# TensorE's order in the first mixer written by hand: the recurrent heads and the attention become stages that advance between the contraction steps of the projections

## The chip, the core and the metric

The kernel runs on one core of one Trainium2 chip. The metric is device time in microseconds (us) of one execution, from three runs. Five engines matter: TensorE (PE) multiplies, VectorE (DVE), ScalarE (ACT) and GpSimd (POOL) work on vectors, and SyncE (SP) issues most of the DMAs (ACT issues the rest). Each takes its instructions strictly in order. An instruction whose data are not there holds up everything behind it on its engine.

## The reference, cut to what matters

A diffusion backbone of two layers over 256 latent tokens and 256 context tokens, 2048 features, in f32. The first layer's mixer has eight heads of a recurrent memory (gated delta rule, in chunks of 64, both directions of time) and beside them eight heads of attention to a neighbourhood on a grid; one input projection feeds both, one output projection takes both. The second layer's mixer is a short convolution. A gated feed-forward block follows each. The change lies in the first mixer.

```python
# gated delta rule, per chunk: M from k and decay, T = inverse of (I + M)
m = where(i > j, einsum(kb, k) * decay, 0)
t_inv = triangular_solve(eye + m, eye)
u = t_inv @ (v * beta);  w = t_inv @ (kb * exp(gc))
def step(s, xc):                       # from chunk to chunk, state s
    v_new = u_c - w_c @ s
    s_next = s * exp(gl_c) + kd_c.T @ v_new
    o_c = qd_c @ s + a_c @ v_new       # latent tokens only
```

k, q and v of these heads go through a convolution over five tokens and SiLU first. k and q are then scaled to length one and rotated. The context tokens are scanned first; their final state starts the scan of the latent tokens. The attention heads add a relative bias, and the recurrent heads' outputs are normalised and gated with a projection z.

## The kernel before, in words

**Projections as streams.** f32 products are made of three products of reduced-precision parts: a weight is split into whi (ACT, L170) and wlo (DVE L238 for the first 576 columns of 1024, POOL L240 for the rest), an activation into a high and a low part. A *stream* is one projection: it loads weights by SP (L227, tile raw), splits them, and for each of 16 contraction steps of 128 features issues its matmuls. `fm_stream` (L308) puts features on the partitions, with matmuls 256 wide: 24 in a step where latent and context tokens are both projected, 12 where only latent tokens are. `tm_stream` (L279, L280, L282) puts tokens on the partitions, with matmuls 512 wide: 12 in a step. The streams of the first mixer come in this order: KA0, KA1 (k of the recurrent heads, four heads each), QA0, QA1 (q), VA0, VA1 (v), QB0, QB1, KB0, VB0, KB1, VB1 (q, k, v of the attention), ZA (the gate z), WO0, WO1 (the output projection). In the profile shown they start at about 110, 147, 204, 244, 281, 341, 390, 428, 466, 534, 605, 688, 748, 853 and 930 us; WO1 ends at 978.5.

**Deferred work.** After a projection of recurrent heads, `head_evac` (L568) puts ten items into the list `later`; `drive` (L411) takes one from it after each contraction step of the next stream. `front` runs the convolution (ACT, then four steps on DVE at L560, SiLU on ACT at L562; tile cv). `back` turns its result with matmuls against an identity (L189, tile sm, four of 128x128), copies it (L170, tile hq), squares it on POOL (L590) and sums on DVE (L591). `done` makes the reciprocal roots (L213 to L218) and runs `normalise` on POOL (L606 scaling, L612 to L615 rotation) and DVE (L616, L617). For k it then writes the tile to memory (L630, kd). For q it turns it to features with L189 matmuls (`sm<-cs,hq`) and writes these.

**Recurrent heads.** `gates` makes decay factors. `chunk_matrices` loads k back from kd (L779, tile ktok), turns it (`gd<-cs,ktok`, L189), forms the products and decay masks (POOL L768 tile gm, PE L772, ACT L774 tile em, DVE L808 tile nt) and solves small triangular systems on DVE. `inverses` joins these into larger blocks on PE (L883, L896). `scan` carries the state (PE L921, L930, L941, L949, L963; DVE L924 tile R; ACT L945 tile vd, L959 tile vn). `latent_scores` makes the matrix AT (L996, L997). In the code all of this stands as straight calls: `chunk_matrices` and `inverses` ahead of QA0, the scans and `latent_quad` ahead of QB0.

**Attention.** `na_scores` loads a bias strip (issued by ACT, L1084, tile br with one buffer), adds a band mask on POOL (L1087, tile bq) and makes scores (L1091 and L1092). `na_values` turns the probabilities (L189, tile PT) and multiplies with v (L1115). Its tiles take the room of the context activations, which VB1 is the last to read. Eight heads, ahead of ZA in the code.

**Who orders the work.** A scheduler with a model of each instruction's time takes the whole program and orders every engine's instructions; the order in the code is only the order of the dependences. One thing is held: the first turning matmul of each convolved head keeps its place (`keep_in_program_order`, L586). Beside the streams a `Pump` advances jobs for modulation weights (`ada_job`; ACT L332, POOL L333, DVE L335) at rates R_QB, R_KB, R_ZA, R_WO per step.

## Time and profile before

| what | value |
|---|---|
| median of three runs | 2942.07 us (2934.33, 2942.07, 2943.47) |
| profiled execution, its own time | 2944.36 us |
| its span, first to last instruction | 2942.5 us |
| mean granted TensorE clock | 0.981 of full speed |
| first mixer from the start of KA1 to the end of WO1 | 146.7 to 978.5 us |

The rows that the prediction shows are read like this. In a window's row stand its length, then busy time and number of instructions of PE, PEld (weight loads), DVE, ACT and POOL, then the granted clock, the share of time in which the DMA engines were busy, and GB/s. In a row of waits stand engine, tile and line of what waited, what it waited for, the sum in us, how often, and the longest. In a timeline row stand start, duration, engine, line, operation, written and read tiles, shapes, count, and in brackets the idle time ahead of it and what ended it. In a group's row stand count, then busy time and mean ns of one, then idle time ahead. The matmuls of PE overlap: one's duration is longer than the distance to the next. An engine name with a q (ACTq, SPq) is a DMA's issue.

### The profile page before, as it was taken

Reading aid. Unit: us, or ns where it says so; the run is one execution under the profiler, and the core shown is the slowest. Engines: PE = TensorE matmul, PEld = TensorE weight load, DVE = VectorE, ACT = ScalarE, POOL = GpSimd, SP = SyncE. Lnnn points to the kernel's source line nnn. Section 1 sums busy time; section 2 is a strip of 40 time slices with the busy share of each in tenths; the row PEclk is TensorE's granted clock in tenths of the full one; section 3 lists DMA queues with packets and bytes.
Section 4 is the critical chain, followed back from the end, with each engine's and each line's share of the span. In section 5 each row is a group of like instructions: output and inputs, shape, how many; then the busy total and the mean of one; then the engine's idle time right before and its main releaser. Section 6 shows DMA issues by size and latency. Waiting matters only on the chain. (4 is left out here: it accounts for less than half of the span.)

```text
span 2942.5 us, 40694 instructions
## 1 busy us (share of the span) xinstructions
PE 2757.0 (94%) x15113; PEld 2292.6 (78%) x15113; DVE 1896.3 (64%) x2409; ACT 1335.1 (45%) x1822; POOL 587.1 (20%) x431
## 2 busy tenths in 40 slices
PE   5898998989899999999999999999999999999997
PEld 3688988878777778878877777777777888888886
DVE  3378766845566777666667867777767446445675
ACT  3245544333354444444445555453544444444554
POOL 1147535336322111110111101111101001000010
PEclk9999999999999999999999999999999999999999
DMA  9954567777767688877878766878568667656653
GB/s 344 297 156 115 159 196 242 240 225 222 218 191 245 236 290 287 301 265 260 274 252 274 261 198 239 296 259 301 196 193 294 194 186 257 187 186 217 191 193 122
DMA packets 284929, 680.80 MB, mean 231 GB/s; under 512 B 57273, under 2 KB 97313, under 8 KB 283323
## 3 DMA queue, kind: packets, MB, share of 16 engines
q1 hardware_dynamic: 262148, 652.48, 67.5%
q10 hardware_dynamic: 22583, 25.73, 2.9%
q8 instruction: 118, 1.93, 0.3%
q14 instruction: 80, 0.66, 0.1%
HBM read 657.63 MB, written 20.48 MB: 230 GB/s over the span
## 5 line engine op out<-in xcount | busy, mean ns | idle before, releaser
L238 DVE TENSOR_TENSOR wlo<-raw,whi 128x1024 fp32r<-128x1024 f32 (+1 forms) x800 | 1009.2, 1274 | 490.1 <-ACT whi L170 476.8
L170 ACT ACTIVATE whi<-raw 128x1024 fp32r<-128x1024 f32 x800 | 835.7, 1055 | 634.3 <-PE mm L282 449.5
L335 DVE SCALAR_TENSOR_TENSOR acc<-araw,cT,acc 128x1024 f32<-128x1024 f32 (+1 forms) x312 | 357.5, 1146 | 292.7 <-DMA araw<-in_ada_w_dram 252.4
L280 PE MATMUL mm<-wlo,fhi 128*128 128x512 f32 x1232 | 478.8, 394 | 3.6 <-DVE wlo L238 3.3
L279 PE MATMUL mm<-whi,fhi 128*128 128x512 f32 x1232 | 476.4, 397 | 0.0
L282 PE MATMUL mm<-whi,flo 128*128 128x512 f32 x1232 | 394.1, 393 | 0.0
L333 POOL TENSOR_TENSOR acc<-araw,acc 128x1024 f32<-128x1024 f32 (+1 forms) x78 | 155.7, 1996 | 1118.0 <-ACT araw L332 632.3
L280 PEld LDWEIGHTS mm<-wlo,fhi 128*128 128x128 f32 x1232 | 232.9, 189 | 57.8 <-DVE wlo L238 8.4
L282 PEld LDWEIGHTS mm<-whi,flo 128*128 128x128 f32 x1232 | 232.2, 189 | 50.2
L279 PEld LDWEIGHTS mm<-whi,fhi 128*128 128x128 f32 x1232 | 233.1, 189 | 48.6 <-ACT sg L1262 0.4
L279 PE MATMUL mm<-whi,ahi 128*128 128x512 f32 x672 | 262.1, 395 | 3.8 <-ACT ahi L173 2.0
L280 PE MATMUL mm<-wlo,ahi 128*128 128x512 f32 x672 | 261.8, 393 | 0.3 <-DVE wlo L238 0.3
L240 POOL TENSOR_TENSOR wlo<-raw,whi 128x448 fp32r<-128x448 f32 x112 | 160.2, 1432 | 279.8 <-ACT whi L170 259.8
L282 PE MATMUL mm<-whi,alo 128*128 128x512 f32 x672 | 211.5, 395 | 2.1 <-DVE alo L174 1.7
L332 ACT ACTIVATE araw<-araw,cT 128x1024 f32<-128x1024 f32 (+1 forms) x78 | 74.4, 954 | 301.0 <-DMA araw<-in_ada_w_dram 256.8
L308 PE MATMUL mm<-hllo,whi 128*128 128x256 f32 x640 | 184.6, 291 | 0.0
L308 PE MATMUL mm<-hlhi,wlo 128*128 128x256 f32 x600 | 172.1, 291 | 4.5 <-DVE wlo L238 4.5
L308 PE MATMUL mm<-hlhi,whi 128*128 128x256 f32 x600 | 170.2, 293 | 1.2 <-DVE hlhi L506 1.2
L1159 POOL TENSOR_TENSOR xs<-rtmp,xs 128x512 f32<-128x512 f32 x24 | 35.4, 1496 | 631.4 <-DVE rtmp L1157 631.4
L279 PEld LDWEIGHTS mm<-whi,ahi 128*128 128x128 f32 x672 | 126.8, 189 | 32.2 <-ACT ahi L173 2.8
L282 PEld LDWEIGHTS mm<-whi,alo 128*128 128x128 f32 x672 | 126.2, 189 | 32.2 <-DVE alo L174 5.1
L280 PEld LDWEIGHTS mm<-wlo,ahi 128*128 128x128 f32 x672 | 126.7, 189 | 29.4 <-DVE wlo L238 1.9
(398 smaller groups left out, 4677.6 us busy)
## 6 DMA issues: line engine op xcount, KB each, us to landing
araw<-in_ada_w_dram SPq DMA_DIRECT2D x288, 512.0 KB
raw<-in_ffn_w_down_dram SPq DMA_DIRECT2D x176, 512.0 KB
raw<-in_ffn_w_gate_dram SPq DMA_DIRECT2D x160, 512.0 KB
raw<-in_ffn_w_up_dram SPq DMA_DIRECT2D x160, 512.0 KB
raw<-in_ev_w_in_dram SPq DMA_DIRECT2D x112, 512.0 KB
araw<-in_ada_w_dram SPq DMA_DIRECT2D x192, 256.0 KB
raw<-in_od_w_in_dram SPq DMA_DIRECT2D x96, 512.0 KB
raw<-in_ev_w_out_dram SPq DMA_DIRECT2D x32, 512.0 KB
```

Source lines behind the costliest of these rows:

```text
L170: ACT.activation(dst, src, AF.Copy)
L238: DVE.tensor_tensor(lo[:, 0:cut], raw[:, 0:cut], hi[:, 0:cut], op=OP.subtract)
L240: POOL.tensor_tensor(lo[:, cut:], raw[:, cut:], hi[:, cut:], op=OP.subtract)
L279: PE.matmul(ps[ti][n], a, hi[:, n * 512:(n + 1) * 512], start=first, stop=False)
L280: PE.matmul(ps[ti][n], a, lo[:, n * 512:(n + 1) * 512], start=False, stop=False)
L282: PE.matmul(ps[ti][n], b, hi[:, n * 512:(n + 1) * 512], start=False, stop=last)
L308: PE.matmul(ps[f][:, n * 256:(n + 1) * 256], wt, mv(w, k), start=False, stop=i == len(ks) - 1 and g == len(group) - 1 and j == 2 and w == ...
L332: ACT.activation(raw, raw, AF.Copy, scale=col)
L333: POOL.tensor_tensor(acc2, raw, acc2, op=OP.add)
L335: DVE.scalar_tensor_tensor(acc, raw, col, acc, op0=OP.mult, op1=OP.add)
L1159: eng.tensor_tensor(v, tmp, v, op=OP.add)
```

## The change

From the end of KA0 to the end of WO1, PE's instructions keep the order in which the code issues them (`tc.manual_schedule` for PE alone); the scheduler still orders the other engines. To set that order, the code is rewritten:

- `gates`, `chunk_matrices`, `inverses`, `scan`, `latent_scores` and `latent_quad` become generators that yield between stages, joined in `recurrent`. `drive` advances this chain by `pace` stages after each contraction step: 0.5 during KA1, 0.55 during QA, 0.8 during VA, 0.5 during QB, 1.1 during KB and VB. What is left when VB1 ends is issued there (`chain.finish`).
- In `scan` the two directions of time are issued together in each stage. In `chunk_matrices` and `latent_scores` the mask gm is made a stage ahead of its matmuls.
- The attention becomes a generator, advanced by 1.7 stages in each step of ZA. The loads of a head are issued two heads ahead of its scores, except for head 0 and head 1. Scores, turning and values are stages of their own; the score tiles alternate between the two PSUM pools for every head (GH is gone).
- The recurrent heads' outputs (`latent_out`) become stages in WO (one per step). YO, the order of contraction in WO, is (2, 3, 0, 1) instead of (2, 0, 1, 3).
- The turning of q to features comes three deferred steps later, as two items (`features`).
- The pump's rates: R_KB 1.8 to 1.9, R_ZA 1.8 to 3.0. An `ada_job` of the mixer yields twice more ahead of its own PE work (lag).

The set of instructions is the same; their order differs. The lines of the changed code stand up to 75 further down.

```diff
+S_KA, S_QA, S_VA, S_QB, S_KB, S_ZA, S_WO = 0.5, 0.55, 0.8, 0.5, 1.1, 1.7, 1.0
...
-    def drive(stream, pump=None, n=1):
+    def drive(stream, pump=None, n=1, chain=None, pace=0):
         for _ in stream:
             if later:
                 f, args = later.pop(0)
                 f(*args)
+            if chain:
+                chain(pace)
...
+            for _ in range(3):
+                defer(lambda: None)
             for g in range(2):
+                defer(features, qt, g)
...
+    order = Stack()
+    order.enter_context(tc.manual_schedule(engines={mybir.EngineType.PE}))
...
             ktok = load_tok("ktok", kd, t0, q)
             kT = g4("kT", "kT").rearrange("p (h t) -> p h t", h=4)
+            yield
             to_features(kT, ktok, gdt)
...
+                gm = [masked(d, t0 + ti, q) for d in range(2)]
+                yield
...
+    def recurrent():
+        yield from gates()
+        parts = yield from chunk_matrices(1)
+        xdTs = []
+        for q in range(2):
+            xdTs.append((yield from inverses(parts, q)))
+        parts = yield from chunk_matrices(0)
+        for q in range(2):
+            yield from scan(q, 1, xdTs[q])
...
+    chain = Pump([recurrent()], 1, 1)
+    drive(fm_stream([(wv, C_KA + 512, 512)], ks, [0, 1], ka_evac(1)), None, 0, chain, S_KA)
...
+    def attention():
+        loads = {0: na_loads(0)}
+        yield
+        loads[1] = na_loads(1)
+        held = na_scores(0, *loads.pop(0))
+        vb = na_values(0)
+        for h in range(8):
+            yield
+            if h < 6:
+                loads[h + 2] = na_loads(h + 2)
+            ahead = na_scores(h + 1, *loads.pop(h + 1)) if h < 7 else None
+            yield
+            PT = na_turned(h, held)
+            vnext = na_values(h + 1) if h < 7 else None
+            yield
+            na_out(h, vb, PT)
+            held, vb = ahead, vnext
```

Three places in the order follow.

**PE, where the second half of the keys comes back** (heads 4 to 7, loaded as ktok). Before, this stands in the stream VA0:

```order
L308 MATMUL mm<-hlhi,whi 128x256
L308 MATMUL mm<-hchi,whi 128x256
L308 MATMUL mm<-hllo,whi 128x256
L189 MATMUL gd<-cs,ktok 128x128 x8
L189 MATMUL sm<-cs,hq 128x128 x6
L308 MATMUL mm<-hclo,whi 128x256
```

Now it stands in QA0. The row of four `sm<-cs,cv` is the last turned head of KA1; 24 stream rows stand between the two rows with gm, and 12 behind the second, of which the last three are shown.

```order
L190 MATMUL sm<-cs,cv 128x128 x4
L824 MATMUL gd<-kT 128x128 x4
L789 MATMUL gd<-cs,gm 128x128 x4
...
L789 MATMUL gd<-cs,gm 128x128 x4
...
L309 MATMUL mm<-hlhi,whi 128x256
L309 MATMUL mm<-hllo,whi 128x256
L309 MATMUL mm<-hlhi,wlo 128x256
L190 MATMUL gd<-cs,ktok 128x128 x8
L309 MATMUL mm<-hlhi,whi 128x256
```

The turning of ktok has moved from VA0, two streams after KA1, to 36 stream matmuls after KA1's last convolved head.

**POOL, at the same keys** (sq are squares, hq the keys, rope the rotation, gm masks, n_... copies for the inverses, wlo the weights' low parts). Before:

```order
L590 TENSOR_TENSOR sq<-hq 128x256
L606 TENSOR_TENSOR hq<-hq,rkr 128x512 x4
L240 TENSOR_TENSOR wlo<-raw,whi 128x448
L612 TENSOR_TENSOR rope<-hq,cs 128x256
L613 TENSOR_TENSOR rope<-hq,cs 128x256
L590 TENSOR_TENSOR sq<-hq 128x256
```

Now:

```order
L595 TENSOR_TENSOR sq<-hq 128x512
L840 COPY n_1845<-nt 32x128 x2
L781 TENSOR_TENSOR gm<-cs,g_t 128x512 x2
L241 TENSOR_TENSOR wlo<-raw,whi 128x448
L840 COPY n_1845<-nt 32x128 x2
L611 TENSOR_TENSOR hq<-hq,rkr 128x512 x4
L617 TENSOR_TENSOR rope<-hq,cs 128x256
L618 TENSOR_TENSOR rope<-hq,cs 128x256
```

The scaling of these keys now comes directly behind their own last squares with two masks, a weight's low part and four copies between; before, it stood among the squares of the queries (128x256), a stream later.

**PE, at the start of ZA** (kb, qb and bq are an attention head's keys, queries and bias). Before:

```order
L1091 MATMUL sm<-kb,qb 128x512 x2
L279 MATMUL mm<-whi,hlhi 128x512 x4
L949 MATMUL gd<-vd,ktok 128x128 x2
L280 MATMUL mm<-wlo,hlhi 128x512
L949 MATMUL gd<-vd,ktok 128x128
...
L963 MATMUL gd<-vn,AT 128x128 x4
L1092 MATMUL sm<-bq,cs 128x256 x2
```

Now, after the first 24 matmuls of ZA:

```order
L1163 MATMUL gd<-kb,qb 128x512
L1164 MATMUL gd<-bq,cs 128x256
L1163 MATMUL sm<-kb,qb 128x512
L1164 MATMUL sm<-bq,cs 128x256
L1163 MATMUL gd<-kb,qb 128x512
L1164 MATMUL gd<-bq,cs 128x256
L1163 MATMUL sm<-kb,qb 128x512
L1164 MATMUL sm<-bq,cs 128x256
L345 MATMUL sm<-cs,acc 128x1 x4
L280 MATMUL mm<-whi,hlhi 128x512
```

The scores of head 0 and of head 1 now stand in one group with no stream matmul between, and the last steps of the scan have moved ahead of ZA.

## The prediction

> **What bounds the kernel now.** I read the page first:

> ```profile
> PE 2757.0 (94%) x15113; PEld 2292.6 (78%) x15113; DVE 1896.3 (64%) x2409; ACT 1335.1 (45%) x1822; POOL 587.1 (20%) x431
> ```

> TensorE is busy for 94% of the span, and the change alters none of its work. So only three things can move the end: PE's idle time, its clock, and work of others that comes too late for it. The windows of the first mixer say how much there is. They are cut at KA1 to VA, QB to VB, and ZA to WO:

> ```profile
> 146.70:389.50 242.80, 224.92 (x1803) 221.32 (x1802) 192.91 (x340) 119.69 (x180) 134.28 (x130) 0.96 0.48 144
> 389.50:748.40 358.90, 321.37 (x3067) 293.58 (x3066) 225.35 (x365) 131.94 (x231) 165.36 (x138) 0.97 0.74 227
> 748.40:978.50 230.10, 213.91 (x1041) 171.75 (x1039) 148.17 (x253) 107.14 (x188) 63.41 (x49) 0.98 0.72 226
> ```

> Length less PE's busy time gives 17.9, 37.5 and 16.2 us of idle time, 71.6 us together. The clock column adds 242.8 × 0.04 + 358.9 × 0.03 + 230.1 × 0.02 = 25 us at most. So nothing can be worth more than 97 us, 3.3% of the span. PE's waits in the same windows name what it waits for. First part:

> ```profile
> PE sm L189 <- ACT cv L562: 12.6, 8, 2.8
> PE mm L308 <- DVE wlo L238: 1.7, 1, 1.7
> PE sm L698 <- ACT abs L170: 1.5, 1, 1.5
> PE gd L189 <- DMA ktok<-kd: 1.5, 1, 1.5
> ```

> Middle:

> ```profile
> PE gd L941 <- ACT state L170: 3.9, 1, 3.9
> PE gd L772 <- DVE AT L997: 3.3, 1, 3.3
> PE gd L941 <- DVE R L924: 3.0, 1, 3.0
> ...
> PE gd L772 <- POOL gm L768: 2.3, 3, 0.8
> ```

> End:

> ```profile
> PE sm L1092 <- POOL bq L1087: 2.7, 1, 2.7
> PE sm L1115 <- ACT PT L165: 2.6, 2, 1.8
> ...
> PE gd L930 <- DMA qT<-qTd: 1.2, 1, 1.2
> ```

> No wait is longer than 4 us. The scheduler puts a step of the heads where its data are there, and the idle time is many small misses. The change swaps this for a fixed order, so the sum asks two things at each place: how long is the chain of other engines, and how much PE work stands between its start and its end.

> **The prices of a matmul.** At the start of QB the timeline of PE shows both clocks:

> ```profile
> 402.50 1.22 PE L308 MATMUL mm<-hlhi,wlo 128*128 128x256 f32 x4 [2.83 <-DVE wlo L238]
> ...
> 403.74 0.41 PE L308 MATMUL mm<-hllo,whi 128*128 128x256 f32 x1
> 403.95 0.41 PE L308 MATMUL mm<-hlhi,wlo 128*128 128x256 f32 x1
> ...
> 405.80 0.28 PE L308 MATMUL mm<-hlhi,wlo 128*128 128x256 f32 x1
> 405.92 0.28 PE L308 MATMUL mm<-hlhi,whi 128*128 128x256 f32 x1
> 939.64 0.39 PE L279 MATMUL mm<-whi,yhi 128*128 128x512 f32 x1
> 939.88 0.39 PE L280 MATMUL mm<-wlo,yhi 128*128 128x512 f32 x1
> ```

> From start to start a matmul of 256 takes 0.12 us, and 0.21 after the wait of 2.83 us; from 402.5 to 405.8, 3.3 us, it runs slow. One such window loses 3.3 × (1 − 0.12/0.21) = 1.4 us. A matmul of 512 takes 0.23 to 0.24. A contraction step is thus 24 × 0.12 = 2.9 us (feature streams of 512 tokens), 1.4 us (256 tokens), or 12 × 0.23 = 2.8 us (token streams).

> **First part: keys and queries of the recurrent heads.** The longest chain of other engines leads from a projection's last convolved head to the use of its keys. For KA0 the timelines show it:

> ```profile
> 175.90 0.66 PE L189 MATMUL sm<-cs,cv 128*128 128x128 f32 x4 [2.62 <-ACT cv L562]
> 176.70 0.58 ACT L170 ACTIVATE hq<-sm 128x512 f32<-128x512 f32 x1
> 177.97 1.04 POOL L590 TENSOR_TENSOR sq<-hq 128x512 f32<-128x512 f32 x1
> 183.36 0.68 DVE L591 TENSOR_REDUCE hss<-sq 128x4 f32<-128x512 f32 x1
> 188.39 5.07 POOL L606 TENSOR_TENSOR hq<-hq,rkr 128x512 f32<-128x512 f32 x4
> 194.53 0.75 POOL L612 TENSOR_TENSOR rope<-hq,cs 128x256 f32<-128x256 f32 x1
> 199.17 1.19 POOL L612 TENSOR_TENSOR rope<-hq,cs 128x256 f32<-128x256 f32 x1 [0.70 <-DVE hq L617]
> L630 ACTq DMA_DIRECT2D kd<-hq x2: 544/588/633, 206.8 to 292.8; - x2
> L189 PE MATMUL gd<-cs,ktok x16: 272/348/476, 215.8 to 304.4; 128*128 128x128 f32 x16
> ```

> From 175.9 to 215.8 are 39.9 us. Taken apart: turning 0.66, copy 0.58, squares 1.04, from the sum to the scaling 188.39 − 183.36 = 5.03, scaling 5.07, first rotation 199.17 − 194.53 = 4.6, second 206.8 − 199.17 = 7.6, writing to memory and loading back 215.8 − 206.8 = 9.0. That is 33.6 us; the other 6.3 are other work ahead in DVE's and POOL's order. The two rotations also hold two of the weights' low parts on POOL (about 1.2 and 1.6). Without these the chain is 30.8 us.

> For KA1's keys the new order puts, between the last `sm<-cs,cv` and `gd<-cs,ktok`, 36 stream matmuls and three small groups of four: 36 × 0.12 + 3 × 1.1 = 7.7 us. (A group with gm is 27.2 us / 24, the row is below.) Nothing else can run on PE: its order is fixed. POOL's new order helps the chain, since the scaling directly follows the squares, but two masks, one low part and four copies lie in the 5 us in which the sum is made. So here PE waits about 30.8 − 7.7 = 23 us, where it waited for nothing. Lower bound: the rotations at POOL's bare time (8 × 0.75 = 6) and 2 us from sum to scaling give 24.4 − 7.7 = 17; upper: KA0's whole 39.9 − 7.7 = 32. SP is stuck behind this ktok load too, with the weights queued behind it; PE waits anyway, and the loads go on when it does. I take **+23**.

> [...]

> KA0's keys come back after 192 matmuls of KA1, the gates' few, and 24 of QA0: 216 × 0.12 + 1.2 = 27.1 us. The wait is 30.8 − 27.1 = 3.7 to 39.9 − 27.1 = 12.8; I take **+8**.

> For the queries the turning to features stands a fixed distance behind their last head. Before:

> ```profile
> 326.09 0.44 PE L189 MATMUL sm<-cs,cv 128*128 128x128 f32 x2 [2.05 <-ACT cv L562]
> 342.92 0.38 PE L189 MATMUL sm<-cs,hq 128*128 128x128 f32 x2
> ```

> That is 16.8 us for QA1. The new order has 60 matmuls of QA1 between for QA0 (7.2 us) and 120 of VA0 for QA1 (14.4 us): 9.6 + 2.4 = **+12**. If the chain is 5 us longer, +22; if it is 12 us, +5.

> Of the old waits, those for wlo, abs and ktok go (−4.7), and I let half of the 12.6 for the convolution go, since steps of the chain now stand in between (−6; 0 to −12.6). First part: 23 + 8 + 12 − 4.7 − 6 = **+32** (+9 with every short value and all of the 12.6 gone, +60 with every long one).

> **Middle: the scans.**

> ```profile
> L772 PE MATMUL gd<-cs,gm 128*128 128x128 f32 x192 | 27.2, 287 | 6.0 <-DVE AT L997 3.3 <-POOL gm L768 2.5 <-ACT em L774 0.2
> L924 DVE SCALAR_TENSOR_TENSOR R<-gd,negegc,vtok 128x128 f32<-128x128 f32 x48 | 13.4, 341 | 6.4 <-PE gd L921 3.3 <-DMA vtok<-vd__139 3.1
> L945 ACT ACTIVATE vd<-gd,brest 128x128 f32<-128x128 f32 x48 | 13.6, 367 | 7.2 <-PE mm L290 4.4 <-PE gd L941 2.3 <-ACT nst L165 0.5
> ```

> A stage now handles both directions, so eight R (8 × 0.341 = 2.7 us) or eight vd (2.9 us) are made between one stage and the next, and one contraction step of 2.8 to 2.9 us lies there. That is about even: with anything else in DVE's or ACT's order, PE waits a little. The masks gm are a stage ahead, so their 2.3 us go. The four rows shown hold 12.5 us, the rest of the 37.5 are scattered waits of a like kind. I let 15 go. Bounds: 0, if small misses only change place; −33, if all go but the weight's 2.8 and the pump's. **−15.**

> **End: attention.** The bias of a head is a chain as well:

> ```profile
> 751.00 0.71 ACTq L1084 DMA_DIRECT2D br<-in_ev_rpb_dram  x1
> 762.19 1.28 ACTq L1084 DMA_DIRECT2D br<-in_ev_rpb_dram  x2
> 760.62 1.10 POOL L1087 TENSOR_TENSOR bq<-br,cs 128x384 f32<-128x384 f32 x1 [1.79 <-DMA br<-in_ev_rpb_dram]
> 773.07 0.99 POOL L1087 TENSOR_TENSOR bq<-br,cs 128x384 f32<-128x384 f32 x1 [5.35 <-DMA br<-in_ev_rpb_dram]
> ```

> br cannot be loaded before VB1 has ended (748.4), and has one buffer. Head 0's bias is ready 761.7 − 748.4 = 13.3 us into ZA, head 1's 774.1 − 761.7 = 12.3 later. Before, steps of the scan and more of ZA's stream filled this time. Now 24 matmuls (5.6 us) and the first key product (0.6) stand ahead of head 0's bias, so PE waits 13.3 − 6.2 = 7. Head 1's scores follow at once, behind some 2 us of score matmuls: 12.3 − 2 = 10. Together +17; if both cycles take the issue-to-sum time of the first alone (10.7), 4.5 + 8.7 = +13. From head 2 on the loads are two heads ahead, over 10 us, and hidden. Probabilities: the order has no stream matmul between turning and values in three heads; at the 1.3 us of the PT row that is 3.9, against 2.6 before. Gone: the old bq wait, 2.7, the 1.2 for qT, and a quarter of the remaining 9.7 that no row here names, 2.8 (0 to 7). **End: 17 + 1.3 − 6.7 = +12** (+2 to +20).

> YO and the pump's rates move work on SP, DVE and POOL that has room (DVE 64% busy, POOL 20%): nothing, up to 3 us either way. For the clock I take 0: four long waits bring some 1.4 us each, as many short ones go.

> **Sum.** +32 − 15 + 12 = +29. Against the profiled execution's own time, 2944.36, that is 2973; this lies 2.3 above the median, so the forecast for the median is 2942.1 + 29 = **2971 us**, 1.0% slower.

> **The rivals.**

> *Faster.* The middle is longest, and a fixed order with a full step between stages may empty it: −33, and with the waits gone the slow windows there, −9. If the keys' chain is at its bounds too (first part +17 + 4 + 5 − 4.7 − 6 = +15) and the biases cost nothing net, the sum is −27: **2915**. It wins as soon as middle and clock save more than the first part adds. For it: 37.5 us of idle time in the middle. Against it: 23 us at one place, from rows.

> *No difference.* First part at +9, end +8, middle −17: **2942**. The chains then run at POOL's bare time.

> *The clock.* The trace shows half speed after a wait of 2.83 us and for 3.3 us. If only waits of a full window's length cause it, cutting up the small ones cures nearly all of the 25 us bound, and the few long waits bring little back: −15 on top of the sum, **2956**, still slower. [...] The 2.83 us wait above is shorter and the clock fell all the same, so I give it little.

> *Much slower.* The fixed order misses at most stages, since 2.9 us of cover barely equal 2.7 to 2.9 of work: the middle doubles to 75 us. 32 + 37 + 12 = +81: **3023**.

> That the order does not change as said is no rival; PE's rows show it.

> **How the numbers follow.** Forecast 0.40, faster 0.27, no difference 0.15, clock 0.09, much slower 0.09. A measurement of this kernel tells about 0.3% from no change (9 us). Faster by more: 0.27. Within: 0.15. Slower: 0.40 + 0.09 + 0.09 = 0.58. The range runs from the faster rival's 2915 to 3003, which is the forecast with first part and end near their long ends (+50, +20) and the middle at −9; beyond it lie half of the much slower case and the part of the faster one with more than 27 us. The forecast's and the clock's own range, with 0.49, is 2950 to 3000.

> **What would show it.** In the changed profile: a wait of about 20 us of `gd` L190 on DMA `ktok<-kd` in QA0; waits of `sm` L190 for hq in QA1; waits of L1164 for bq of 7 and 10 us at ZA's start; the middle window's idle time near 22 us. The prediction is wrong if the ktok wait is under 10 us, or if the middle has under 8 us of idle time left.

## The result, and the profile after

The changed kernel takes 3079.38 us (median of four runs, 3067.96 to 3081.24), against 2938.96 us of the kernel before in the same comparison (four runs, 2934.33 to 2943.47). The ratio is 1.047, with a 95% interval of 1.0437 to 1.0502: 140 us slower, where 29 were forecast, and 76 us beyond the end of the range (3003). The direction was right, the size was off by a factor of five.

The profiled execution's span is 3078.7 us. From its page, the row of busy times and the row of the granted clock:

```profile
PE 2794.9 (91%) x15113; PEld 2324.9 (76%) x15113; DVE 1895.6 (62%) x2409; ACT 1338.1 (43%) x1822; POOL 571.3 (19%) x431
...
PEclk9998899898989899999999999999999999999999
```

The other engines do the same work in the same busy time. TensorE, with the same 15113 instructions, is busy 37.9 us longer, and its clock row has lost tenths in the first third. The windows of the mixer, cut at the same streams as before (KA1 to VA, QB to VB, ZA to WO):

```profile
147.70:461.10 313.40, 246.76 (x2347) 239.91 (x2345) 192.55 (x359) 129.22 (x198) 133.71 (x138) 0.88 0.43 124
461.10:862.40 401.30, 344.31 (x2748) 317.90 (x2748) 232.20 (x408) 138.93 (x264) 153.54 (x130) 0.91 0.62 191
862.40:1126.20 263.80, 207.62 (x817) 159.62 (x815) 137.16 (x187) 90.45 (x133) 59.65 (x49) 0.87 0.65 201
```

Length less PE's busy time gives 66.6, 57.0 and 56.2 us of idle time, 179.8 together against 71.6 before: +108. PE's busy time in the three windows is 798.7 against 760.2: +38.5, for the same matmuls. The sum, 146.7, is what the mixer grew by (978.5 against 831.8). KA1 starts 1.0 later, and behind the mixer the program is 11.5 us shorter (1952.5 against 1964.0), a gain that no run here traces to a cause. PE's waits in the three windows; the first part:

```profile
PE gd L190 <- DMA ktok<-kd: 24.8, 2, 23.5
PE sm L190 <- DVE hq L622: 24.4, 4, 11.1
PE mm L305 <- DVE hst L168: 6.7, 3, 5.0
...
PE sm L190 <- ACT cv L569: 1.8, 1, 1.8
```

The middle:

```profile
PE sm L345 <- POOL acc L338: 18.9, 1, 18.9
PE gd L911 <- DVE xd L927: 5.5, 3, 3.7
PE gd L964 <- DVE R L956: 5.3, 4, 2.1
PE gd L789 <- DVE AT L1026: 3.8, 2, 2.1
```

The end:

```profile
PE gd L1164 <- POOL bq L1156: 10.2, 2, 7.0
PE mm L280 <- ACT whi L171: 9.5, 2, 8.6
PE gd L1193 <- ACT PT L166: 6.8, 1, 6.8
PE sm L1193 <- DVE PT L168: 6.4, 1, 6.4
PE sm L190 <- DVE o_t L1048: 6.3, 3, 5.3
...
PE sm L1193 <- issue: 3.9, 1, 3.9
PE gd L1193 <- issue: 3.2, 1, 3.2
```

Before, no wait of the mixer's windows was longer than 4 us; now there are single waits of 23.5, 18.9, 11.1 and 8.6. PE stands behind one instruction of its fixed order while the streams' matmuls, ready, stand behind it.

**The clock.** PE's timeline behind the longest wait:

```profile
268.19 1.94 PE L190 MATMUL gd<-cs,ktok 128*128 128x128 f32 x8 [23.48 <-DMA ktok<-kd]
...
271.21 0.41 PE L309 MATMUL mm<-hlhi,whi 128*128 128x256 f32 x1
271.42 0.41 PE L309 MATMUL mm<-hllo,whi 128*128 128x256 f32 x1
...
272.56 0.28 PE L309 MATMUL mm<-hllo,whi 128*128 128x256 f32 x1
272.68 0.28 PE L309 MATMUL mm<-hlhi,wlo 128*128 128x256 f32 x1
```

Up to 272.4, for 4.2 us, the granted clock is 0.50 and the stream's matmuls start 0.21 us apart, then, at a granted clock of 1.00, 0.12. Added up over the timeline of the mixer, TensorE works 129.6 us at this pace, against 45.6 before. At the slow pace 1 − 0.12/0.21 = 0.43 of the time is lost. The 84 us more of slow work thus lose 36 us more, which is the 38.5 of busy time but for 2.

### The profile page after: what moved, and what is told of

The parts are those of the page before. It is cut to its first block, busy times and chain, and to the rows that moved or that the text cites. A ratio compares the mean times of both kernels' runs of the same rounds, so it can differ in the third digit from the quotient of the medians.

```text
span 3078.7 us, 40709 instructions
## 1 busy us (share of the span) xinstructions
PE 2794.9 (91%) x15113; PEld 2324.9 (76%) x15113; DVE 1895.6 (62%) x2409; ACT 1338.1 (43%) x1822; POOL 571.3 (19%) x431
## 5 line engine op out<-in xcount | busy, mean ns | idle before, releaser
L239 DVE TENSOR_TENSOR wlo<-raw,whi 128x1024 fp32r<-128x1024 f32 (+1 forms) x800 | 992.8, 1254 | 555.1 <-ACT whi L171 533.7
L336 DVE SCALAR_TENSOR_TENSOR acc<-araw,cT,acc 128x1024 f32<-128x1024 f32 (+1 forms) x312 | 367.1, 1177 | 291.4 <-DMA araw<-in_ada_w_dram 250.0
L280 PE MATMUL mm<-whi,fhi 128*128 128x512 f32 x1232 | 476.0, 396 | 0.0
L280 PEld LDWEIGHTS mm<-whi,fhi 128*128 128x128 f32 x1232 | 232.5, 189 | 48.9 <-ACT sg L1361 0.5
L280 PE MATMUL mm<-whi,ahi 128*128 128x512 f32 x672 | 262.8, 396 | 4.3 <-DVE rtmp L1250 2.3
L333 ACT ACTIVATE araw<-araw,cT 128x1024 f32<-128x1024 f32 (+1 forms) x78 | 74.5, 955 | 268.8 <-DMA araw<-in_ada_w_dram 221.1
L309 PE MATMUL mm<-hlhi,whi 128*128 128x256 f32 x600 | 179.1, 306 | 1.8 <-DVE hlhi L513 1.2
L280 PEld LDWEIGHTS mm<-whi,ahi 128*128 128x128 f32 x672 | 127.5, 190 | 32.9 <-ACT ahi L174 2.8
```

Of the source, the lines that this page charges most:

```text
L239: DVE.tensor_tensor(lo[:, 0:cut], raw[:, 0:cut], hi[:, 0:cut], op=OP.subtract)
L280: PE.matmul(ps[ti][n], a, hi[:, n * 512:(n + 1) * 512], start=first, stop=False)
L309: PE.matmul(ps[f][:, n * 256:(n + 1) * 256], wt, mv(w, k), start=False, stop=i == len(ks) - 1 and g == len(group) - 1 and j == 2 and w == ...
L333: ACT.activation(raw, raw, AF.Copy, scale=col)
L336: DVE.scalar_tensor_tensor(acc, raw, col, acc, op0=OP.mult, op1=OP.add)
```

## The experiments

The two profiles suggest a theory and two rivals. *Cover*: each long wait is a chain of other engines less the stream work that the fixed order puts in its way, and slow clock behind it. *Rewriting*: the generators, paces and pump rates cost by themselves, with TensorE in any order. *Clock*: what idle time does to the clock is a cost of its own, not one window for each wait. All runs were compared with the kernel before beside them (2937.9 to 2938.6 us).

**e1: no hand order.** One line of the changed kernel is taken out.

```diff
-    order.enter_context(tc.manual_schedule(engines={mybir.EngineType.PE}))
```

> The changed kernel without the manual order for TensorE: generators, paces, pump rates, YO and the deferred features stay, the scheduler orders TensorE too. Theory (the fixed order of TensorE makes the waits): the waits for ktok (23.5 us), hq (24.4) and the pump's acc (18.9) go, 2925 to 2960 us. Rival (the rewritten code, above all the pump's rates and the queries' later features, costs by itself): over 3000 us.

Measured: 2985.55 us, ratio 1.0154 (1.0135 to 1.0173). Between the two expectations: the hand order costs 94 of the 140 us, and 47 us are left with none. Its waits from ZA to WO:

```profile
PE sm L345 <- POOL acc L338: 18.2, 2, 10.8
PE sm L345 <- POOL zst L1200: 9.7, 1, 9.7
```

Both are the pump's sums (L345), in the streams for which the change raised the pump's rate or left it at 2.

**e2 and e3: the hand order in one half.** In e2 `order.close()` moves ahead of the attention; in e3 `manual_schedule` is entered there.

```diff
+    order.close()                                   # e2
+    order.enter_context(tc.manual_schedule(...))    # e3
     chain = Pump([attention()], 1, 1)
```

> Hand order only from KA1 to VB1; the scheduler orders TensorE from ZA on. If the two halves add up as the stages of the two profiles say (+114 us up to the start of ZA, +34 from there to the end of WO1, -11 behind it): 3025 to 3050 us. Rival (the attention's waits are the scan's missing cover, and the scheduler fills ZA no better than the hand did): 3065 to 3085 us.

> Hand order only from ZA to the end of WO. If the halves add up: 2955 to 2975 us, with waits for bq, PT and whi as in the changed kernel. Rival (with the scan's last steps free to slide into ZA or the loads of the bias earlier, the attention loses little): 2935 to 2950 us.

Measured: e2 3050.89 us (1.0381; 1.0365 to 1.0396), e3 2991.2 (1.0173; 1.0153 to 1.0193). e2 is just above what the stages said. e3 fits neither expectation. Against e1, the common base without hand order, the order of the heads costs 65 us, that of the attention 6 (the intervals of e1 and e3 overlap, so it may be nothing), and both together 94: the rest, 23, comes only with both. In e3 steps of the recurrence are still there in ZA (it waits 6.1 us for vn there), and could serve the attention as cover. That this makes the 23 is an argument; no run tests it.

**e4 and e11: filling the long waits.** Matmuls that no output uses are put ahead of five of the waiting places; nothing else moves. They multiply parts of the activations that are in place, 0.12 us each. e4 has 400 of them, e11 527; the numbers in the cut are e11's.

```diff
+    def fill(n, p):
+        for _ in range(n):
+            PE.matmul(p[:, 0:256], hs_lo[0][:, 1, 0:128], hs_hi[0][:, 0, :], start=True, stop=True)
...
+            if seq and q:
+                fill(192, smt())
             to_features(kT, ktok, gdt)
...
+                fill((130, 0, 65, 0)[sum(fills)], gdt())
...
+            if lag and seg == 2 and blk == 1:
+                fill(140, gdt())
```

> The changed kernel with 400 matmuls of 256 columns more that no output uses: 150 just ahead of the waiting ktok turning, 70 + 20 + 20 + 20 ahead of the four turnings of q to features, 120 ahead of the pump's second reduction; 0.12 us each, 48 us of added work inside 67 us of waits. Theory (waits over some 2 us make the clock fall, and the slow stretches after these five waits, 22.8 us of work at 0.57 speed, cost 9.8 us): 3065 to 3073 us, no slow stretch behind these places. Rival of the prediction (a wait costs one slow window of 1.4 us at most): 3073 to 3078. Rival (the added matmuls are on the path): 3100 to 3127.

> As e4_fill, with the added matmuls sized to leave each of the long waits under 1 us: 192 ahead of the ktok turning, 130 and 65 ahead of the first turning of q to features of each query half, 140 ahead of the pump's second sum (527 in all, 63 us of work that no output uses). Theory (what makes the clock fall is the idle time itself, over half of one 3.4 us window): the slow stretches behind these places go, 15 to 20 us of work at 0.57 speed, 3066 to 3074 us. Rival (the long waits' clock costs 1.4 us each): 3073 to 3077. Rival (the added work delays the path): 3085 and more.

Measured: e4 3078.48 us (1.0473; 1.0456 to 1.0490), just above its rival's range, e11 3062.81 (1.0433; 1.0406 to 1.0459), below the 3066 to 3074 of its theory. e4 decides nothing: its fillings left waits of 5.5, 2.8, 4.4, 4.6 and 2.6 us behind them, and behind those of 4.4 and 4.6 the stream's matmuls start 0.21 us apart again. In e11 1.5 us are left at the keys, 1.1 or less at the queries and 2.1 at the pump's sum, and behind the keys' 1.5 the stream's matmuls start 0.12 us apart. (The pump's next sum waits 4.7 us, where it did not in the changed kernel.) Its timeline at the keys, the same place as above:

```profile
269.01 1.06 PE L190 MATMUL gd<-cs,ktok 128*128 128x128 f32 x8 [1.52 <-DMA ktok<-kd]
...
270.27 0.28 PE L309 MATMUL mm<-hlhi,whi 128*128 128x256 f32 x1
270.39 0.28 PE L309 MATMUL mm<-hllo,whi 128*128 128x256 f32 x1
```

And its window over the mixer:

```profile
147.50:1110.90 963.40, 844.55 (x6434) 762.19 (x6432) 562.64 (x953) 359.75 (x594) 350.23 (x317) 0.94 0.57 175
```

Without the 527 added matmuls (527 × 0.12 = 63.2 us) PE is busy 781.3 us, against 798.7 in the changed kernel: beside 63 us of useless work the necessary work is 17 us shorter. The work at the slow pace explains it: it falls from 129.6 to 89.3 us in the mixer, where the granted clock is 0.94 instead of 0.89, and 40.3 × 0.43 is 17. The time of the whole kernel is less sharp. The medians differ by 16.6 us, the two ratios by 0.0037, which is 11 us; the single runs (3058.0 to 3075.4, against 3068.0 to 3081.2) and the two intervals overlap. So busy time and pace carry the verdict: the clock is a cost of its own, in these two profiles over twice the 1.4 us for each of five waits.

**e5 and e12: what the rewriting costs without hand order.** e5 is e1 with the pump of before. e12 is e5 with the generators advanced faster.

```diff
-R_KB = 1.9
-R_ZA = 3.0
+R_KB = 1.8
+R_ZA = 1.8
...
-    pump = Pump([ada_job(..., lag=2), ...
+    pump = Pump([ada_job(..., lag=0), ...
...
-S_KA, S_QA, S_VA, S_QB, S_KB, S_ZA, S_WO = 0.5, 0.55, 0.8, 0.5, 1.1, 1.7, 1.0
+S_KA, S_QA, S_VA, S_QB, S_KB, S_ZA, S_WO = 0.5, 0.55, 0.9, 0.5, 2.2, 3.4, 2.0    # e12
```

> The kernel without hand order (e1), with the pump of before: R_KB and R_ZA 1.8, no lag. Theory (of the 47 us that e1 lost without any hand order, the waits for the pump's sums, acc, 9.7 + 18.2 us in ZA and WO0, are the most, since R_ZA of 3.0 crowds them there): 2950 to 2962 us. Rival (the loss comes from the other rewriting: paces in which the generators hand out their instructions, both directions in one stage, later queries): 2975 to 2990.

> The kernel without hand order and with the pump of before (e5), its generators advanced faster: 0.9 stages a step instead of 0.8 in VA, 2.2 instead of 1.1 in KB and VB, 3.4 instead of 1.7 in ZA, 2 instead of 1 in WO. Theory (the scheduler prefers what comes first in the code, so the generators' late place in the code holds the heads back, and this is the 27 us that e5 lost): 2942 to 2956 us. Rival (the place in the code does not matter to it; the loss comes from buffers held longer by stages of two directions): 2958 to 2975.

Measured: e5 2965.24 us (1.0096; 1.0064 to 1.0128), between its two expectations, e12 2946.65 (1.0033; 1.0016 to 1.0050), as its theory said. The pump's rates and lag are 20 us of e1's 47, the paces another 19, and 9 us are left, where the kernel before is still the faster. The pace sets only where a step stands in the code, and without hand order the scheduler is free to move it: it evidently does not move it far enough ahead by itself. That the two directions in a stage hold buffers longer can cost little more than these 9 us, since e12 keeps them.

**e6: more cover for keys and queries.** Eight empty stages ahead of the turning of the second keys; the queries' turning counted from its own list, 12 and 5 steps later.

```diff
             yield
+            if seq and q:
+                for _ in range(8):
+                    yield
             to_features(kT, ktok, gdt)
...
-            for _ in range(3):
-                defer(lambda: None)
             for g in range(2):
-                defer(features, qt, g)
+                waits.append([4 + (12, 5)[q] + g, features, (qt, g)])
```

> The changed kernel with eight empty stages ahead of the turning of the second keys (216 instead of 36 stream matmuls behind the last convolved head of KA1) and the queries' turning 12 and 5 contraction steps later. Theory (each wait is its chain less the stream work that stands between): the ktok wait falls from 23.5 to about 5 us, the hq waits from 24.4 to 0 to 3, slow stretches of 15 us of work behind them go: 3025 to 3040 us. Rival (all later stages of the recurrence move back eight stages, and the waits come back there or behind VB1): 3055 to 3085.

Measured: 3039.98 us (1.0338; 1.0306 to 1.0370), 39 less than the changed kernel and at the end of the range that its theory gave. The first part's waits:

```profile
PE mm L305 <- DVE hst L168: 16.6, 6, 6.4
PE gd L190 <- DMA ktok<-kd: 13.5, 2, 12.3
```

The queries' waits are gone, those for hst are 10 us longer. The keys still wait 12.3, not 5, with 216 matmuls in between. Where the chain starts, with KA1's last convolved head, is in PE's timeline, and where it writes its result in the view of the tile kd (the later of the two starts). Of the changed kernel:

```profile
235.52 0.60 PE L190 MATMUL sm<-cs,cv 128*128 128x128 f32 x4
```

```profile
L635 ACTq DMA_DIRECT2D kd<-hq x2: 539/583/627, 211.0 to 260.1; - x2
```

and of e6, with the timelines of POOL and DVE between:

```profile
233.00 0.60 PE L190 MATMUL sm<-cs,cv 128*128 128x128 f32 x4
```

```profile
L646 ACTq DMA_DIRECT2D kd<-hq x2: 544/589/634, 209.1 to 274.7; - x2
```

```profile
246.73 5.07 POOL L622 TENSOR_TENSOR hq<-hq,rkr 128x512 f32<-128x512 f32 x4 [0.38 <-DVE rkr L219]
251.76 1.31 POOL L241 TENSOR_TENSOR wlo<-raw,whi 128x448 fp32r<-128x448 f32 x1
...
258.23 1.23 POOL L631 TENSOR_TENSOR hq<-hq,cs 128x256 f32<-128x256 f32 x1
```

```profile
258.80 3.85 DVE L578 SCALAR_TENSOR_TENSOR cv<-hst,evcT,cv 128x254 f32<-128x254 f32 x6
...
264.05 0.41 DVE L632 TENSOR_TENSOR hq<-hq,rope 128x256 f32<-128x256 f32 x1
```

From start to write the chain takes 24.6 us in the changed kernel and 41.7 in e6. The stream that serves as cover brings work of its own. It needs its weights' low parts from POOL, which does six of them (8.0 us) between the scaling and the end of the second rotation; and its heads need their convolution from DVE (L578), behind which the rotation's next step (L632) starts at 264.05, though POOL was done with its part at 259.5. Cover does not come free; here it lengthened the chain that it was to hide.

**e7: the pump's rates.** R_QB 0.6 for 1.2, R_ZA 1.8 for 3.0, in the changed kernel.

> The changed kernel with R_QB 0.6 instead of 1.2 and R_ZA 1.8 instead of 3.0. Theory (the wait of 18.9 us for acc in QB1 stands there because the pump places the sum's matmuls before its weights can have come, and the 8.6 us for whi at the start of WO0 because SP has the pump's loads ahead of WO's weights): both go, 3040 to 3055 us. Rival (the pump's sums are late wherever they stand, and its work then falls into WO): 3065 to 3085.

Measured: 3069.29 us (1.0443; 1.0413 to 1.0472), in the range of its rival and not in the theory's 3040 to 3055. The wait of 18.9 us in QB1 is gone (QB1 takes 31 us instead of 52), but the waits from QB0 on are:

```profile
PE sm L345 <- POOL acc L338: 13.0, 2, 7.7
PE sm L1193 <- ACT PT L166: 11.7, 2, 10.9
PE mm L280 <- ACT whi L171: 10.6, 2, 9.6
```

The pump's sums wait elsewhere, 13.0 us of them, and the weights at the start of WO come no sooner, so the pump's rate in ZA was not what held them. What does stays open. In both traces SP issues WO's first weights (at 1005.2 us in the changed kernel, at 978.2 in e7) behind loads of the pump; in the changed kernel SP waited 11.5 us for POOL (acc, L324) and 4.9 for DVE (acc, L336) from 985 us to there; no run took these loads away.

**e8: two buffers for the bias strip.**

```diff
-        br = nap.tile([128, 6, 64], F32, name="br", tag="br", bufs=1)
+        br = nap.tile([128, 6, 64], F32, name="br", tag="br", bufs=2)
```

> The changed kernel with two buffers for the bias strip br. Theory (ACT issues the strip's loads and stands in them until br is free; the copies PT and the exponentials queue behind): the PT waits of 20 us fall under 8 and the second bq wait of 7.0 under 2, 3055 to 3066 us. Rival (the PT waits are there because no stream matmul stands between turning and values): 3072 to 3082.

The reason for it is in ACT's timeline of the changed kernel, in ZA:

```profile
907.75 0.60 ACTq L1153 DMA_DIRECT2D br<-in_ev_rpb_dram  x1
908.40 0.60 ACT L166 ACTIVATE PT<-gd 128x512 f32<-128x512 f32 x1 [5.90 <-POOL bq L1156]
```

ACT stands 5.9 us before the issue of a strip's load, since br is not free until POOL has made bq; the copy PT that PE waits for (6.8 us) is next in its queue. Measured: 3066.24 us (1.0425; 1.0390 to 1.0461), just at the end of the expected range; the interval reaches into that of the changed kernel. The waits in ZA are now:

```profile
PE sm L1193 <- issue: 12.6, 2, 7.6
PE mm L280 <- ACT whi L171: 9.9, 2, 9.1
PE gd L1164 <- POOL bq L1156: 5.1, 1, 5.1
...
PE gd L1193 <- ACT PT L166: 1.8, 1, 1.8
```

The second bq wait, 7.0, is gone as expected; the first is 5.1 instead of 3.2. The waits ahead of L1193 add up to 14.4 instead of 20.3, where under 8 were expected. For two of them, 12.6, the profile names no releaser, but in DVE's timeline each ends as soon as DVE has made its half of PT (at 903.8 and 958.9 us). Ahead of the first, ACT's exponential stood behind a step of the pump (L333) that had waited 5.57 us for its weights, and DVE's half behind another (L336) that had waited 3.62. So the strip's buffer was one cause of the PT waits and not the whole.

**e9 and e10: the repairs together.** e9 joins e6, e7 and e8; e10 is e9 with the hand order ending where ZA begins.

> All three repairs in the changed kernel together: keys and queries later (e6), pump rates (e7), two bias strips (e8). If the repairs add (-39, -10, -13 us): 3010 to 3025 us. Rival (a slow clock ends only when waits grow rare, so the repairs together bring more than their sum): 2985 to 3005.

> As e9_all, with the hand order ending where ZA begins. Theory (what the hand order costs behind ZA, 28 us in e2, is there beside the repairs): 2982 to 3000 us. Rival (pump and bias repairs acted in that very part, so little is left): 3003 to 3015. Below 2951 would mean that the hand order of the heads is harmless once its cover is right.

Measured: e9 3025.04 us (1.0278; 1.0250 to 1.0305), e10 3010.96 (1.0249; 1.0226 to 1.0272). The repairs come to 54 us of the 62 of their sum: no recovery beyond the sum. e10 has its rival's value. With all three repairs in, and only the heads in hand order, the kernel is still 73 us behind the kernel before. This is not the price of the hand order alone: the rewriting is in it (27 us in e5, without hand order), and so are waits that no repair removed (12.6 us for the second keys). No version here beats the kernel before.

## Why the prediction was wrong

Four steps failed: the clock, taken as 0; the pump, taken to have room; the middle, of which 15 were to go; and the chains of the queries and of PT, priced by rows of their old places. The steps, as forecast and as measured. Idle time is from PE's wait rows and windows of the two profiles, in us.

| step | forecast | measured |
|---|---|---|
| second keys (ktok, 36 matmuls of cover) | +23 | 23.5 |
| first keys | +8 | 1.3 |
| queries to features | +12 | 24.4 |
| convolution's waits eased | -6 | -10.8 |
| first window, idle | +32 | +48.7 |
| middle window, idle | -15 | +19.5 |
| of it the pump's sum | 0 | 18.9 |
| bq | +14.3 (17 - 2.7) | +7.5 |
| PT (all waits of L1193) | +1.3 | +17.7 |
| weights at WO's start, and o_t | in no term | 15.8 |
| last window, idle | +12 | +40.0 |
| clock | 0 | +38.5 |
| behind the mixer, and KA1's start | 0 | -10.5 |
| sum | +29 | +136 of span |

**What held.** The method held where it was applied to a whole chain: the second keys were forecast at 23 us from rows of another place and waited 23.5. Part of this closeness is luck. From the last turning (235.52) to the use (268.19) the chain took 32.7 us where 30.8 were taken, and 9.2 lay in between instead of 7.7. In POOL's timeline the scaling of these keys is

```profile
249.22 4.03 POOL L611 TENSOR_TENSOR hq<-hq,rkr 128x512 f32<-128x512 f32 x4 [0.38 <-DVE rkr L219]
```

so the way to it took 13.7 us where the sum has 7.3, since masks, low parts and copies lie in it; the rest, 19.0 us, is 4.5 shorter than in the sum (scaling 4.0 for 5.1, rotations 6.9 for 9.4, writing and loading back 8.1 for 9.0). These errors nearly cancel. That the kernel would be slower followed from such counts, but 47 us of it came from the rewriting (e1), which was in no term. Neither sign of being wrong appeared (the keys' wait is not under 10 us, the middle's idle time not under 8): they watched neither the clock nor the pump. Of the rivals, the one called much slower came nearest, with 3023 and a middle of 75 us where 57.0 were measured. Two small slips in the sums change nothing: a quarter of 9.7 is 2.4, not 2.8, and the first part's long values add up to 62, not 60.

**"For the clock I take 0."** This was the largest miss, 38.5 us. The step took 1.4 us for each long wait and set the vanishing short ones against it. The runs showed that a slow stretch can go on while small waits keep coming (one of 13.7 us had only 3.3 us of idle time in it), and that filling five waits gives 17 us of busy time back (e11). As a rival the clock stood in the text with the wrong sign: it was to bring a gain.

**"YO and the pump's rates move work on SP, DVE and POOL that has room: nothing, up to 3 us either way."** This looked at the share of busy time of engines, not at the matmuls that the pump itself puts into PE's fixed order. One of them waited 18.9 us in QB1. The weights for its sum come through three buffers, and most of them are freed by DVE's steps of the sum (L336). DVE had these among the steps of the triangular solve (L865, L867), and so SP waited with the next loads. SP's waits from 498 to 545 us:

```profile
SPq L328 <- DVE zsol L867: 6.4, 5, 2.6
...
SPq L328 <- DVE acc L336: 3.8, 2, 3.6
```

PE stood from 525.6 on. The last three loads for the sum were issued at 535.4, 537.3 and 538.3, and POOL's last step for it ended at 544.5, when PE went on:

```profile
539.29 1.33 POOL L334 TENSOR_TENSOR acc<-araw,acc 128x512 f32<-128x512 f32 x1 [10.76 <-ACT araw L333]
543.15 1.32 POOL L338 TENSOR_TENSOR acc<-acc,acc 128x512 f32<-128x512 f32 x1 [2.53 <-issue]
```

So DVE had no room at this place: it was busy for 28.3 of the 29 us from 514 to 543. e7 confirms the place, e1 and e5 that the rates cost even without hand order (20 us), and e7 also that slower rates in the fixed order mostly move the wait.

**"The middle: I let 15 go."** Without the pump's wait the middle window has 38.1 us of idle time, against 37.5. So nothing went: the bound "small misses only change place" was the right one. A step of 2.9 us between stages of 2.7 to 2.9 us of work removed some waits (state 3.9, gm 2.3) and left others (R 5.3, xd 5.5, AT 3.8).

**PT at "1.3 us in three heads".** The waits were 6.8, 6.4, 3.9 and 3.2. The step priced the copy by a row of before, and did not ask what stands ahead of it on ACT and DVE. For the first wait it was a DMA's issue on ACT that waited for a buffer (e8). The loads "two heads ahead", taken as hidden, were what put it there. For the second, at 928.8, it was on DVE a step of the pump's sum that waited for its weights, with the softmax and the copy behind it:

```profile
919.25 1.26 DVE L336 SCALAR_TENSOR_TENSOR acc<-araw,cT,acc 128x512 f32<-128x512 f32 x1 [5.54 <-DMA araw<-in_ada_w_dram]
...
927.97 0.68 DVE L168 COPY PT<-gd 128x512 f32<-128x512 f32 x1
```

**First keys and bias.** Here the forecast was too high. The bias waits are 3.2 and 7.0 us instead of 7 and 10. The first keys wait 1.3 instead of 8; ahead of them PE now stands 6.1 us for hst (at 211.6 and 215.0), which was in no term, and this counts as cover too. Nor was there a term for the 9.5 us that wait for WO's weights and the 6.3 for o_t.

**Queries.** 16.8 us was the chain's length in its old place, and the waits are twice what it gave: 15.5 for the first half and 8.9 for the second, where 9.6 and 2.4 were forecast. In DVE's timeline of the changed kernel the chain's rotation (L621, L622) now stands between steps of the triangular solve (L865, L867), which began at 344.2 before the change, behind the queries' turning at 342.9:

```profile
319.05 0.42 DVE L621 TENSOR_TENSOR hq<-hq,rope 128x256 f32<-128x256 f32 x1
319.38 0.35 DVE L865 TENSOR_TENSOR sub_tmp<-lsol,zsol 128x192 f32<-128x192 f32 x1
```

How much of the lengthening is this was not tried by itself. e6 shows the like for the keys: a chain's length is not a constant, it changes with the work that runs beside it.

## What to carry to other kernels

A fixed order of one engine is priced chain by chain: work that stands between, against the length of the chain on the other engines in the same company, for every instruction that the order pins, those of background jobs and those behind a DMA's issue among them. A chain measured beside other work than it will have is only an estimate: the keys' took 39.9 us in KA0's place, 32.7 in its new one, and 51.8 in e6, where more work ran beside it. And idle time of TensorE is not paid once: here 108 us more of it in the mixer came with 84 us more of work at the slow pace, which lost 36 us. Count these slow windows too.

## What the runs showed of the hardware that I had not expected

In e11 useless matmuls made the useful ones faster: with 63 us of them in otherwise idle time the same other matmuls were busy 17 us less, and the kernel's median was 16.6 us lower (11 by the ratios).
